# An encoder kernel's inner norms: second statistics as sums and squares, more late modulation units ahead of the norm, and constants loaded later

## The chip, the cores and the metric

The kernel runs on one core of a Trainium2 chip. The metric is the device time of one execution in microseconds (us), the median of several runs. The engines are TensorE (PE in the profile, PEld for its weight loads), VectorE (DVE), ScalarE (ACT), GpSimd (POOL) and SyncE (SP), whose queue issues most of the DMA transfers. Each takes its own list of instructions.

## The reference

Two layers of an encoder for 256 tokens of 2048 columns, all in float32. Cut to what matters here:

```python
for l in range(2):
    mod = (silu(c) @ w_mod[l] + b_mod[l]).reshape(bn, 6, d)       # shift_m, scale_m, gate_m, shift_f, scale_f, gate_f
    h = layer_norm(x) * (1.0 + scale_m) + shift_m
    proj = h @ w_in[l]                                            # 4288 columns
    y_a, y_b, y_c, y_d = ...                                      # gMLP, latent attention, short conv, conformer conv
    y = concatenate([y_a, y_b, y_c, y_d]) @ w_out[l]
    x = layer_norm(ALPHA * x + (1.0 + gate_m) * y, post_mix_g[l], post_mix_b[l])
    h = layer_norm(x) * (1.0 + scale_f) + shift_f
    y = conv_ffn(h, w_up, w_conv, b_conv, w_down)                 # 2048 -> 2 x 5632 -> 2048
    x = layer_norm(ALPHA * x + (1.0 + gate_f) * y, post_ffn_g[l], post_ffn_b[l])
```

At the end of each half of a layer two layer norms follow each other: one with gain and bias that makes the new x, and at once a plain one that makes the input of the next half. The second needs the mean and the variance of what the first has written. I call the three places where both follow each other the inner norms: o0 (after layer 0's output projection), d0 (after layer 0's feed-forward) and o1 (after layer 1's output projection). After d1 only the first norm is left, and the output is stored.

## The kernel before

**Products.** The weights come from memory in tiles of 1 MB (`raw`, a ring of four, `weights()`). A tile is split into a rounded part and a remainder, in fp32r: ScalarE casts `whi` (or `thi`), VectorE subtracts `wlo` (or `tlo`), and TensorE makes three products for each pair. The activations are split likewise (`hT`, `a`). Where a call says `exact`, the weights are loaded into the places of the halves instead (`wexact`), and TensorE makes one fp32 product, which it does in two records; ScalarE and VectorE then have nothing to do. In `out_proj` of layer 0, `plain={1024: 2, 1536: 4}` says which units are exact: two of the four of the column block at 1024, and all four of the block at 1536.

**Order.** `stream()` issues the load of one unit and puts its products off until after the load of the next. The order on each engine follows the order of the code, as a scheduler settles it from dependences; each engine then runs its list in order.

**Modulation.** `c @ w_mod` is made by VectorE (`mod_step`: one multiply-add per 128 rows, into `macc` or `qacc`) and summed over the partitions by TensorE (`ps_mod`). It goes on in the background: after each unit of weights `pump()` adds the rate of the phase (`RATES`) to a credit, and takes that many units of `mod_stream`. Layer 0's SHIFT_F and SCALE_F are first done up to column 1536; their last 512 columns are the eight late units (four of SHIFT_F, four of SCALE_F, each with 1 MB and four operations of 128x512). Before the change they begin after the norm o0: `load_late_first()` loads the first two into slots, and the rest follow in the phase "first". `needs()` settles the sums, `late()` those of the late columns.

**The start.** x is loaded and normed, and layer 0's SHIFT_M and SCALE_M are made in five pieces of columns (`piece()`, `PIECES`), while the products D, U, V and E use the columns that are done (`by_pieces()`). The constants `cst` beyond the first 128 columns and the parameter rows (`load_rows`, ten transfers of at most 64 KB) are issued on GpSimd's queue at the very start. The rows are turned by TensorE (`ps_rows`) after the second piece.

**The inner norms.** `out_proj` ends with a block of 512 columns, whose last four units are put off: TensorE makes their products for token tile 0 (128 tokens) first, then for tile 1. So the norm of tile 0 (`finish`, then `norm`) runs under the products of tile 1. For each tile VectorE multiplies with the gate (`yg`, L692), adds the residual (L695), takes statistics (L698), and then passes over the four quarters of x: `(x - mean) * gain` (L715), `* rstd + bias` (L718), and `bn_stats` of the result (L724). `rstd_of` makes the mean and 1/std of these second statistics (L562, L564, GpSimd's power on L112, L567), the pair r. From r ScalarE makes `xn` (L86), TensorE transposes it (`ps_xT`), ScalarE (tile 0) or VectorE (tile 1) writes `hF` with scale and shift, and the products of the next half begin (`first_group`: `g_c` after o0 and o1, `U_c` after d0).

Of the kernel before, what the change touches and what calls it, by code (L numbers as in the profile page):

```python
# [13 lines left out]
P = 128  # L14
# [40 lines left out]
def encoder_kernel(ctx: ExitStack, tc: tile.TileContext, A: dict, consts: bass.AP, out: bass.AP):  # L55
# [52 lines left out]
    mhalf = keep.tile([P, 4], F32, name="mhalf")  # L108
    pool.memset(mhalf, -0.5)

    def power(o, i):
        pool.tensor_tensor(out=o, in0=i, in1=mhalf[:, : i.shape[1]], op=ALU.pow)  # L112

# [11 lines left out]
    cact = keep.tile([P, 16], F32, name="cact")  # L125
    dve.tensor_copy(cact, pst[:, 0:16])

    def load_rows(parts, n, dst):

        r = smallp.tile([P, P], F32, tag="rows", name="rows", bufs=5)  # L130
        at = 0
        for ap in parts:
            pool.dma_start(out=r[at : at + ap.shape[0], :], in_=ap)
            at += ap.shape[0]
        assert at == n

        def turn():
            ps = ms_tile("ps_rows")
            pe.transpose(ps[:, 0:n], r[0:n, :], ident[0:n, 0:n])
            dve.tensor_copy(dst, ps[:, 0:n])  # L140

        return turn

    def rows(ap):
        if len(ap.shape) == 1:
            return ap.rearrange("(j p) -> j p", p=P)
        return ap.rearrange("k (j p) -> (k j) p", p=P)
# [4 lines left out]
        bcol.append(b)  # L152
    turn_b0 = load_rows([rows(A["b_mod"][0])], 96, bcol[0])

    pool.dma_start(out=cst[:, 128:1024], in_=consts[:, 128:1024])

    PM = []
    PF = []
    for l in range(DEPTH):
# [2 lines left out]
        PM.append(pm)  # L162
        PF.append(pf)

    def load_params(l):
        turns = []
        if l > 0:
            turns.append(load_rows([rows(A["b_mod"][l])], 96, bcol[l]))
        turns.append(load_rows([rows(A["conf_w_dw"][l])], 124, PM[l][:, 0:124]))
        turns.append(  # L170
            load_rows(
                [
                    rows(A["mla_q_norm"][l]),
                    rows(A["mla_kv_norm"][l]),
                    rows(A["sconv_w"][l]),
                    rows(A["conf_b_dw"][l]),
                    rows(A["conf_ln_g"][l]),
                    rows(A["conf_ln_b"][l]),
                ],
                29,  # L180
                PM[l][:, 124:153],
            )
        )
        wc = rows(A["ffn_w_conv"][l])
        turns.append(load_rows([wc[0:128]], 128, PF[l][:, 0:128]))
        turns.append(load_rows([wc[128:132], rows(A["ffn_b_conv"][l])], 48, PF[l][:, 128:176]))
        return turns


# [120 lines left out]
        )  # L310
        return [dst[:, k * 512 : (k + 1) * 512] for k in range(nk)]

    late_first = {}

    def load_late_first():
        for v in (SHIFT_F, SCALE_F):
            late_first[v] = late_part(0, v, 0, 2, slot("wlate")) + late_part(0, v, 2, 2, slot("wlate"))

    def mod_stream(order):

        held_back = {}
        for l, m in order:
            if (l, m) == (0, GATE_F):

                for u in range(4):
                    for v, acc in held_back.items():
                        ws = late_first[v] if u == 0 else late_part(u, v, 0, 4, raw_tile("wmod"))
                        for k in range(4):  # L330
                            mod_step(acc[:, LATE_KT * P :], ws[k], 4 * u + k, u + k == 0)
                        if u == 3:
                            late.append((0, v, acc, LATE_KT, KT))
                        yield
# [319 lines left out]
    def out_proj(l, w, src, order, gate_of, name, post_g, post_b, before, then, plain={}, bg=0):  # L654
# [45 lines left out]
        def gains():  # L700
            gb = []
            for row in (post_g, post_b):
                r = raw_tile("gb")
                nc.sync.dma_start(out=r, in_=row.partition_broadcast(P))
                gb.append(r)
            box["gb"] = gb

        def norm(t):
            gb = box["gb"]
            mv, r = rstd_of(stats[t], f"{name}p{t}", False)  # L710
            st2 = new_stats(f"{name}q{t}")
            for q in range(4):
                cols = slice(q * 512, (q + 1) * 512)
                xs = X[t][:, cols]
                dve.scalar_tensor_tensor(  # L715
                    out=xs, in0=xs, scalar=mv[:, 0:1], in1=gb[0][:, cols], op0=ALU.subtract, op1=ALU.mult
                )
                dve.scalar_tensor_tensor(  # L718
                    out=xs, in0=xs, scalar=r[:, 0:1], in1=gb[1][:, cols], op0=ALU.mult, op1=ALU.add
                )  # L720
                if then is None:
                    nc.sync.dma_start(out=out[0, t * P : (t + 1) * P, cols], in_=xs)
                else:
                    dve.bn_stats(out=st2[:, q, :], in_=xs)  # L724
            if then is not None:
                _, box[t] = rstd_of(st2, f"{name}r{t}", True)

        for c0, width in CHUNKS:
            last = c0 + width == D
# [722 lines left out]
    for l in range(DEPTH):  # L1452
# [4 lines left out]
        else:  # L1457
# [97 lines left out]
```

## Time and profile before

| | |
|---|---|
| median of 3 runs | 2304.81 us (2304.12 to 2306.32) |
| the profiled execution | 2308.31 us, its span 2306.5 us |
| TensorE, busy share of the span | 97% |
| VectorE | 78% |
| ScalarE | 46% |
| GpSimd | 2% |
| mean granted clock of TensorE | 0.987 |

The profile comes from one execution. A row of the timeline reads: start (us from the span's start), duration, engine, line, operation, out<-in, shape, and in brackets how long the engine was idle before it and what ended that. A row of the list of waits reads: who waited, for whom, total us, times, the longest. A row of a stretch reads: from:to, length, then busy us and (instructions) of PE, PEld, DVE, ACT and POOL, the granted clock, the DMA engines' busy share and GB/s.

### The profile page before, as it was taken

To read this page: it belongs to the slowest core of one execution; us is meant where nothing else is said; L and a number is where in the kernel's file an instruction comes from. 1 tells how busy PE (TensorE), PEld (TensorE's weight loads), DVE (VectorE), ACT (ScalarE), POOL (GpSimd) and SP (SyncE) were. 2 spreads that over 40 slices of the span, in tenths; PEclk is the share of its full clock that TensorE was granted. 3 is DMA by queue.
4 is the path that set the end of the run, shared out by engine and by line. 5 is a ranking of instruction groups with operands and counts; after the bars stand their busy time and mean duration, and the time that the engine had idled before them with its cause. 6 is when DMAs were issued, how large, how long until landed. Compare 5 with 4: busy or idle time off the path is not lost. (4 is left out here: it accounts for less than half of the span.)

```text
span 2306.5 us, 31422 instructions
## 1 busy us (share of the span) xinstructions
PE 2240.3 (97%) x12387; PEld 1937.9 (84%) x12387; DVE 1788.2 (78%) x2181; ACT 1062.5 (46%) x1573; POOL 34.7 (2%) x64
## 2 busy tenths in 40 slices
PE   6899999999999999999999999999999999999998
PEld 4688886688888888888789989879888888888886
DVE  6878987778888888987977799887676555565676
ACT  2235742235454544544445435535454454454553
POOL 1000000000000000000000000000000000000000
PEclk9999999999999999999999999999999999999999
DMA  9999788777889888898857667775766555555554
GB/s 343 353 342 342 270 322 330 262 272 284 305 305 335 295 325 323 298 348 304 317 185 249 207 220 258 281 272 183 250 241 215 184 183 201 184 193 190 184 198 146
DMA packets 228717, 605.21 MB, mean 262 GB/s; under 512 B 14660, under 2 KB 27188, under 8 KB 210900
## 3 DMA queue, kind: packets, MB, share of 16 engines
q1 hardware_dynamic: 227784, 602.30, 73.6%
q8 instruction: 97, 1.59, 0.3%
q0 software_dynamic: 784, 0.90, 0.1%
q14 instruction: 52, 0.43, 0.1%
HBM read 601.05 MB, written 2.10 MB: 261 GB/s over the span
## 5 line engine op out<-in xcount | busy, mean ns | idle before, releaser
L451 ACT CAST whi<-wraw 128x1024 fp32r<-128x1024 f32 (+1 forms) x632 | 643.9, 1043 | 783.2 <-PE g_c L83 210.7
L452 DVE TENSOR_TENSOR wlo<-wraw,whi 128x1024 fp32r<-128x1024 f32 (+1 forms) x632 | 751.2, 1214 | 302.8 <-ACT whi L451 285.4
L83 PE MATMUL d<-whi,a 128*128 128x512 f32 x1344 | 390.0, 391 | 0.9 <-ACT whi L451 0.9
L246 DVE SCALAR_TENSOR_TENSOR macc<-wmod,cact,macc 128x2048 f32<-128x2048 f32 (+2 forms) x174 | 353.8, 2034 | 31.6 <-DMA wmod<-in_w_mod_dram 31.0
L83 PE MATMUL v_c<-hT,whi 128*128 128x512 f32 (+1 forms) x1456 | 343.1, 383 | 0.0
L83 PE MATMUL g_c<-hT,whi 128*128 128x512 f32 (+1 forms) x1344 | 313.3, 380 | 0.0
L83 PEld LDWEIGHTS v_c<-hT,whi 128*128 128x128 f32 x1456 | 264.6, 189 | 48.5
L83 PEld LDWEIGHTS d<-whi,a 128*128 128x128 f32 x1344 | 253.2, 189 | 54.5 <-ACT whi L451 2.2
L83 PEld LDWEIGHTS g_c<-hT,whi 128*128 128x128 f32 x1344 | 243.4, 189 | 43.2
L83 PE MATMUL d<-wlo,a 128*128 128x512 f32 x672 | 234.9, 392 | 1.7 <-DVE wlo L452 1.6
L83 PE MATMUL v_c<-hT,wlo 128*128 128x256 f32 x1400 | 190.7, 283 | 0.0
L83 PEld LDWEIGHTS v_c<-hT,wlo 128*128 128x128 f32 x1400 | 183.2, 191 | 6.6
L83 PE MATMUL g_c<-hT,wlo 128*128 128x256 f32 x1280 | 175.8, 283 | 0.0
L83 PEld LDWEIGHTS g_c<-hT,wlo 128*128 128x128 f32 x1280 | 168.2, 191 | 5.9
L83 PEld LDWEIGHTS d<-wlo,a 128*128 128x128 f32 x672 | 127.0, 189 | 30.0 <-DVE wlo L452 3.6
L471 ACT CAST a<-g 128x512 fp32r<-128x512 f32 x132 | 80.6, 619 | 86.4 <-PE d L83 84.7
L83 PE MATMUL o<-whi,a 128*128 128x512 f32 x384 | 112.3, 397 | 0.8 <-ACT whi L451 0.8
L472 DVE TENSOR_TENSOR a<-g,a 128x512 fp32r<-128x512 f32 x132 | 88.0, 684 | 9.0 <-ACT a L471 9.0
L83 PEld LDWEIGHTS o<-whi,a 128*128 128x128 f32 x384 | 73.2, 191 | 17.3 <-issue 1.2
L83 PE MATMUL D_c<-hT,whi 128*128 128x256 f32 x432 | 82.0, 290 | 2.8 <-ACT hT L471 2.3
L246 DVE SCALAR_TENSOR_TENSOR qacc<-wmod,cact,qacc 128x1024 f32<-128x1024 f32 (+1 forms) x75 | 80.3, 1070 | 2.7 <-DMA wmod<-in_w_mod_dram 0.6
L83 PEld LDWEIGHTS D_c<-hT,whi 128*128 128x128 f32 x432 | 69.5, 197 | 4.7 <-ACT hT L471 2.6
(328 smaller groups left out, 2599.6 us busy)
## 6 DMA issues: line engine op xcount, KB each, us to landing
wraw<-in_ffn_w_up_dram SPq DMA_DIRECT2D x168, 1024.0 KB, 5.1
wmod<-in_w_mod_dram SPq DMA_DIRECT2D x134, 1024.0 KB, 6.5
wraw<-in_ffn_w_down_dram SPq DMA_DIRECT2D x88, 1024.0 KB, 5.2
wraw<-in_w_in_dram SPq DMA_DIRECT2D x33, 1024.0 KB, 5.6
wmod<-in_w_mod_dram SPq DMA_DIRECT2D x64, 512.0 KB, 8.7
wraw<-in_w_out_dram SPq DMA_DIRECT2D x26, 1024.0 KB, 6.9
wmod<-in_w_mod_dram SPq DMA_DIRECT2D x32, 768.0 KB, 7.0
wexact<-in_w_in_dram SPq DMA_DIRECT2D x46, 512.0 KB, 7.1
```

Of the source, the lines that this page charges most:

```text
L83: pe.matmul(o, lhsT, rhs, start=start, stop=stop, skip_group_check=True)
L246: i = dve.scalar_tensor_tensor(out=acc, in0=w, scalar=col, in1=acc, op0=ALU.mult, op1=ALU.add)
L451: act.copy(hi[:, :m], r)
L452: i = dve.tensor_tensor(out=lo[:, :m], in0=r, in1=hi[:, :m].bitcast(F32), op=ALU.subtract)
L471: act.copy(hi, src)
L472: dve.tensor_tensor(out=lo, in0=src, in1=hi.bitcast(F32), op=ALU.subtract)
```

## The change

It has five parts.

1. Inner norms: `second(t)` takes the place of `norm(t)`. The offset pass writes its sum too (`accum_out`), ScalarE squares the result about c and sums the squares (`sq`), and six small operations on VectorE make mean and variance of them. c is minus the mean of the bias row, made by `gains()` from four statistics for each inner norm.
2. `RATES` for layer 0's output projection goes from 1.7 to 1.95. In its twelve units with modulation that is three more units, which are the first three late ones. `load_late_first()` then loads the two that follow these.
3. In layer 0's output projection the two exact units of the block at 1024 are split like others.
4. The rest of `cst` and layer 0's rows are issued on SP's queue at the fourth call of `piece` (made at the start of the third piece), and the rows are turned after the last piece.
5. A constant tile `eps`.

```diff
-    dict(B=1.6, C=1.9, out=1.7, first=1.2, up=0.68, down=0.83),
+    dict(B=1.6, C=1.9, out=1.95, first=1.2, up=0.68, down=0.83),
...
+    eps = keep.tile([P, 1], F32, name="eps")
+    pool.memset(eps, LN_EPS)
...
-    def load_rows(parts, n, dst):
+    def load_rows(parts, n, dst, by=pool):
...
-            pool.dma_start(out=r[at : at + ap.shape[0], :], in_=ap)
+            by.dma_start(out=r[at : at + ap.shape[0], :], in_=ap)
...
-    pool.dma_start(out=cst[:, 128:1024], in_=consts[:, 128:1024])
...
+    LATE_UNITS = [(u, v) for u in range(4) for v in (SHIFT_F, SCALE_F)]
+    late_first, late_taken = {}, []
     def load_late_first():
-        for v in (SHIFT_F, SCALE_F):
-            late_first[v] = late_part(0, v, 0, 2, slot("wlate")) + late_part(0, v, 2, 2, slot("wlate"))
+        n = len(late_taken)
+        for u, v in LATE_UNITS[n : n + 2]:
+            late_first[u, v] = late_part(u, v, 0, 2, slot("wlate")) + late_part(u, v, 2, 2, slot("wlate"))
...
+            if then is None:
+                return
+            st = new_stats(f"{name}b")
+            for q in range(4):
+                dve.bn_stats(out=st[:, q, :], in_=gb[1][:, q * 512 : (q + 1) * 512])
+            mb = smallp.tile([P, 2], F32, tag="mv", name=f"mv_{name}b", bufs=4)
+            dve.bn_aggr(out=mb, in_=st)
+            box["c"] = keep.tile([P, 1], F32, tag="negc", name=f"c_{name}")
+            dve.tensor_scalar(out=box["c"], in0=mb[:, 0:1], scalar1=-1.0, scalar2=None, op0=ALU.mult)
+
+        def second(t):
+            gb, c = box["gb"], box["c"]
             mv, r = rstd_of(stats[t], f"{name}p{t}", False)
-            st2 = new_stats(f"{name}q{t}")
+            sums = smallp.tile([P, 4, 6], F32, tag="stats", name=f"st_{name}q{t}", bufs=4)
             for q in range(4):
...
                 dve.scalar_tensor_tensor(
+                    out=xs, in0=xs, scalar=r[:, 0:1], in1=gb[1][:, cols], op0=ALU.mult, op1=ALU.add,
+                    accum_out=sums[:, q, 0:1],
+                )
+                act.activation(
+                    out=tmp_tile("sq"), in_=xs, func=AF.Square, bias=c, accum_out=sums[:, q, 1:2]
+                )
+            m = smallp.tile([P, 6], F32, tag="m2", name=f"m_{name}{t}")
+            dve.tensor_reduce(out=m[:, 0:1], in_=sums[:, :, 0], axis=AX.X, op=ALU.add)
+            dve.tensor_scalar(out=m[:, 1:2], in0=m[:, 0:1], scalar1=1.0 / D, scalar2=None, op0=ALU.mult)
+            dve.tensor_scalar(out=m[:, 2:3], in0=m[:, 1:2], scalar1=c, scalar2=None, op0=ALU.add)
+            dve.scalar_tensor_tensor(
+                out=m[:, 3:4], in0=m[:, 2:3], scalar=m[:, 2:3], in1=eps, op0=ALU.mult, op1=ALU.subtract
+            )
+            dve.tensor_reduce(out=m[:, 4:5], in_=sums[:, :, 1], axis=AX.X, op=ALU.add)
+            dve.scalar_tensor_tensor(
+                out=m[:, 5:6], in0=m[:, 4:5], scalar=1.0 / D, in1=m[:, 3:4], op0=ALU.mult, op1=ALU.subtract
+            )
+            r = smallp.tile([P, 2], F32, tag="rs", name=f"rs_{name}r{t}", bufs=4)
+            power(r[:, 0:1], m[:, 5:6])
+            last_norm[0] = dve.scalar_tensor_tensor(
+                out=r[:, 1:2], in0=m[:, 1:2], scalar=-1.0, in1=r[:, 0:1], op0=ALU.mult, op1=ALU.mult
+            )
+            box[t] = r
...
-                if then is None:
-                    nc.sync.dma_start(out=out[0, t * P : (t + 1) * P, cols], in_=xs)
-                else:
-                    dve.bn_stats(out=st2[:, q, :], in_=xs)
-            if then is not None:
-                _, box[t] = rstd_of(st2, f"{name}r{t}", True)
+                nc.sync.dma_start(out=out[0, t * P : (t + 1) * P, cols], in_=xs)
...
-                    norm(t)
+                    (norm if then is None else second)(t)
...
-            turns.extend(load_params(0))
+        if q == 3:
+            nc.sync.dma_start(out=cst[:, 128:1024], in_=consts[:, 128:1024])
+            turns.extend(load_params(0, nc.sync))
...
-            if q == 1:
+            if q == 4:
                 for turn in turns:
                     turn()
...
-            plain={1024: 2, 1536: 4} if l == 0 else {},
+            plain={1536: 4} if l == 0 else {},
```

Where the instructions stand now is seen at three places. First ScalarE at the inner norm o1, before the change: behind the last cast of the projection's weights come `xn` of tile 0 (x0) and its `hF`.

```order
L451 CAST whi_12542<-wraw_12536 128x1024
L86 ACTIVATE xn_12728<-x0_95,rs_o1r0_12674 128x512
L86 ACTIVATE xn_12739<-x0_95,rs_o1r0_12674 128x512
L86 ACTIVATE hF0_12546<-ps_xT_12730,mod_1_3_6182,mod_1_4_7424 128x128 x4
L86 ACTIVATE hF1_12547<-ps_xT_12741,mod_1_3_6182,mod_1_4_7424 128x128 x4
```

The same place after the change (`sq` are the squares, `st_o1q0` and `st_o1q1` the sums of the two tiles):

```order
L742 ACTIVATE sq_12767,st_o1q0_12764<-x0_97,c_o1_12609 128x512
L742 ACTIVATE sq_12771,st_o1q0_12764<-x0_97,c_o1_12609 128x512
L742 ACTIVATE sq_12775,st_o1q0_12764<-x0_97,c_o1_12609 128x512
L742 ACTIVATE sq_12779,st_o1q0_12764<-x0_97,c_o1_12609 128x512
L742 ACTIVATE sq_12803,st_o1q1_12800<-x1_98,c_o1_12609 128x512
L742 ACTIVATE sq_12807,st_o1q1_12800<-x1_98,c_o1_12609 128x512
L742 ACTIVATE sq_12811,st_o1q1_12800<-x1_98,c_o1_12609 128x512
L742 ACTIVATE sq_12815,st_o1q1_12800<-x1_98,c_o1_12609 128x512
L86 ACTIVATE xn_12849<-x0_97,rs_o1r0_12788 128x512
L86 ACTIVATE xn_12860<-x0_97,rs_o1r0_12788 128x512
L86 ACTIVATE xn_12887<-x0_97,rs_o1r0_12788 128x512
L86 ACTIVATE hF0_12651<-ps_xT_12851,mod_1_3_6253,mod_1_4_7495 128x128 x4
```

The eight squares stand ahead of the first `xn`, those of tile 1 (x1) too, and a third `xn` of tile 0 stands ahead of its first `hF`. It is the same at o0 and d0.

Second, VectorE at the same norm, tile 0, before the change:

```order
L715 SCALAR_TENSOR_TENSOR x0_95<-x0_95,mv_o1p0_12654,gb_12502 128x512 x2
L718 SCALAR_TENSOR_TENSOR x0_95<-x0_95,rs_o1p0_12656,gb_12504 128x512 x2
L724 BN_STATS st_o1q0_12659<-x0_95 128x6 x2
L562 BN_AGGR mv_o1r0_12672<-st_o1q0_12659 128x2
L564 TENSOR_SCALAR rs_o1r0_12674<-mv_o1r0_12672 128x1
L567 SCALAR_TENSOR_TENSOR rs_o1r0_12674<-mv_o1r0_12672,rs_o1r0_12674 128x1
L692 TENSOR_TENSOR yg_12678<-o1_153610_12521,gate_1_2_12163 128x512
```

and after it:

```order
L733 SCALAR_TENSOR_TENSOR x0_97,st_o1q0_12764<-x0_97,rs_o1p0_12761,gb_12600 128x512 x2
L746 TENSOR_REDUCE m_o10_12781<-st_o1q0_12764 128x1
L747 TENSOR_SCALAR m_o10_12781<-m_o10_12781 128x1
L748 TENSOR_SCALAR m_o10_12781<-m_o10_12781,c_o1_12609 128x1
L749 SCALAR_TENSOR_TENSOR m_o10_12781<-m_o10_12781,eps_95 128x1
L752 TENSOR_REDUCE m_o10_12781<-st_o1q0_12764 128x1
L753 SCALAR_TENSOR_TENSOR m_o10_12781<-m_o10_12781 128x1
L758 SCALAR_TENSOR_TENSOR rs_o1r0_12788<-m_o10_12781,rs_o1r0_12788 128x1
L697 TENSOR_TENSOR yg_12791<-o1_153610_12626,gate_1_2_12259 128x512
```

The statistics are gone, small operations have come, and `yg` of tile 1 follows directly behind tile 0's last small operation as before.

Third, SP's queue between the last weights of E in the second piece and the first of D in the third, before the change:

```order
L429 DMA wexact_480<-in_w_in_dram 128x2x512
L437 DMA wraw_527<-in_w_in_dram 128x2x1024
L261 DMA wmod_537<-in_w_mod_dram 128x2x512 x2
L261 DMA wmod_542<-in_w_mod_dram 128x2x512 x2
L261 DMA wmod_547<-in_w_mod_dram 128x2x512 x2
```

and after it:

```order
L434 DMA wexact_455<-in_w_in_dram 128x2x512
L1463 DMA cst_82<-in_consts_dram 128x896
L136 DMA rows_503<-in_conf_w_dw_dram 124x128
L136 DMA rows_505<-in_mla_q_norm_dram 3x128
L136 DMA rows_505<-in_mla_kv_norm_dram 2x128
L136 DMA rows_505<-in_sconv_w_dram 12x128
...
L136 DMA rows_514<-in_ffn_w_conv_dram 4x128
L136 DMA rows_514<-in_ffn_b_conv_dram 44x128
L442 DMA wraw_517<-in_w_in_dram 128x2x1024
```

Eleven transfers have come between E's weights and `wraw`, and the modulation weights of the third piece follow behind them.

More of the change, by code (lines that the diff above doesn't have):

```diff
@@ L163, in encoder_kernel, with load_params @@
         PF.append(pf)
-    def load_params(l):
+    def load_params(l, by=pool):
         turns = []
         if l > 0:
-            turns.append(load_rows([rows(A["b_mod"][l])], 96, bcol[l]))
-        turns.append(load_rows([rows(A["conf_w_dw"][l])], 124, PM[l][:, 0:124]))
+            turns.append(load_rows([rows(A["b_mod"][l])], 96, bcol[l], by))
+        turns.append(load_rows([rows(A["conf_w_dw"][l])], 124, PM[l][:, 0:124], by))
         turns.append(
@@ L181, in load_params @@
                 PM[l][:, 124:153],
+                by,
             )
@@ L184, in load_params @@
         wc = rows(A["ffn_w_conv"][l])
-        turns.append(load_rows([wc[0:128]], 128, PF[l][:, 0:128]))
-        turns.append(load_rows([wc[128:132], rows(A["ffn_b_conv"][l])], 48, PF[l][:, 128:176]))
+        turns.append(load_rows([wc[0:128]], 128, PF[l][:, 0:128], by))
+        turns.append(load_rows([wc[128:132], rows(A["ffn_b_conv"][l])], 48, PF[l][:, 128:176], by))
         return turns
@@ L311, in late_part @@
         return [dst[:, k * 512 : (k + 1) * 512] for k in range(nk)]
-    late_first = {}
+    LATE_UNITS = [(u, v) for u in range(4) for v in (SHIFT_F, SCALE_F)]
+    late_first, late_taken = {}, []
     def load_late_first():
-        for v in (SHIFT_F, SCALE_F):
-            late_first[v] = late_part(0, v, 0, 2, slot("wlate")) + late_part(0, v, 2, 2, slot("wlate"))
+        n = len(late_taken)
+        for u, v in LATE_UNITS[n : n + 2]:
+            late_first[u, v] = late_part(u, v, 0, 2, slot("wlate")) + late_part(u, v, 2, 2, slot("wlate"))
     def mod_stream(order):
@@ L325, in mod_stream @@
             if (l, m) == (0, GATE_F):
[L327 to L334, printed above, removed]
+                for u, v in LATE_UNITS:
+                    acc = held_back[v]
+                    late_taken.append((u, v))
+                    ws = late_first.get((u, v)) or late_part(u, v, 0, 4, raw_tile("wmod"))
+                    for k in range(4):
+                        mod_step(acc[:, LATE_KT * P :], ws[k], 4 * u + k, u + k == 0)
+                    if u == 3:
+                        late.append((0, v, acc, LATE_KT, KT))
+                    yield
             while len(late) >= 2:
@@ new lines, in second @@
+        def second(t):
+            gb, c = box["gb"], box["c"]
+            mv, r = rstd_of(stats[t], f"{name}p{t}", False)
+            sums = smallp.tile([P, 4, 6], F32, tag="stats", name=f"st_{name}q{t}", bufs=4)
+            for q in range(4):
+                cols = slice(q * 512, (q + 1) * 512)
+                xs = X[t][:, cols]
+                dve.scalar_tensor_tensor(
+                    out=xs, in0=xs, scalar=mv[:, 0:1], in1=gb[0][:, cols], op0=ALU.subtract, op1=ALU.mult
+                )
+                dve.scalar_tensor_tensor(
+                    out=xs,
+                    in0=xs,
+                    scalar=r[:, 0:1],
+                    in1=gb[1][:, cols],
+                    op0=ALU.mult,
+                    op1=ALU.add,
+                    accum_out=sums[:, q, 0:1],
[7 more added lines that the diff above has]
+            dve.tensor_scalar(out=m[:, 2:3], in0=m[:, 1:2], scalar1=c, scalar2=None, op0=ALU.add)
+            dve.scalar_tensor_tensor(
+                out=m[:, 3:4], in0=m[:, 2:3], scalar=m[:, 2:3], in1=eps, op0=ALU.mult, op1=ALU.subtract
+            )
+            dve.tensor_reduce(out=m[:, 4:5], in_=sums[:, :, 1], axis=AX.X, op=ALU.add)
+            dve.scalar_tensor_tensor(
+                out=m[:, 5:6], in0=m[:, 4:5], scalar=1.0 / D, in1=m[:, 3:4], op0=ALU.mult, op1=ALU.subtract
[4 more added lines that the diff above has]
+                out=r[:, 1:2], in0=m[:, 1:2], scalar=-1.0, in1=r[:, 0:1], op0=ALU.mult, op1=ALU.mult
+            )
+            box[t] = r
```

## The prediction

> **What bounds the kernel.** I read the page's busy shares first, then the list of waits of TensorE alone, then the timeline around the places that this list names.
>
> ```profile
> span 2306.5 us, 31422 instructions
> PE 2240.3 (97%) x12387; PEld 1937.9 (84%) x12387; DVE 1788.2 (78%) x2181; ACT 1062.5 (46%) x1573; POOL 34.7 (2%) x64
> ```
>
> TensorE (PE) works 97% of the span. Only three things can change the time: its work, its clock, and the some 66 us in which it stands idle. The waits say where it stands (line, what ended the wait, total us, times, longest):
>
> ```profile
> PE ps_xT L1397 <- ACT xn L86: 13.0, 2, 12.8
> PE ps_xT L585 <- ACT xn L86: 9.0, 5, 3.1
> PE E L83 <- DMA wexact<-in_w_in_dram: 4.4, 1, 4.4
> PE ps_mod L83 <- DVE macc L246: 2.2, 1, 2.2
> ```
>
> The first row is the kernel's start. The second is the inner norms (o0, d0, o1), which stop TensorE for 3.1 us at most: the norm of token tile 0 runs under the tail products of token tile 1, and the norm of tile 1 under the first products of tile 0. The change touches every one of these four rows.
>
> **The inner norms: what now releases TensorE.** The norm o1 in the timeline, VectorE and GpSimd, then ScalarE, then TensorE:
>
> ```profile
> 1540.79 0.69 DVE L692 TENSOR_TENSOR yg<-o,gate 128x512 f32<-128x512 f32 x1 [1.93 <-PE o L83]
> ...
> 1543.34 1.40 DVE L715 SCALAR_TENSOR_TENSOR x<-x,mv_o1p,gb 128x512 f32<-128x512 f32 x2
> 1544.66 1.41 DVE L718 SCALAR_TENSOR_TENSOR x<-x,rs_o1p,gb 128x512 f32<-128x512 f32 x2
> 1545.98 1.28 DVE L724 BATCH_NORM_STATS2 st_o1q<-x 128x6 f32<-128x512 f32 x2
> ...
> 1551.43 0.15 DVE L564 TENSOR_SCALAR rs_o1r<-mv_o1r 128x1 f32<-128x1 f32 x1
> 1552.26 0.16 DVE L567 SCALAR_TENSOR_TENSOR rs_o1r<-mv_o1r,rs_o1r 128x1 f32<-128x1 f32 x1 [0.67 <-POOL rs_o1r L112]
> 1552.34 0.69 DVE L692 TENSOR_TENSOR yg<-o,gate 128x512 f32<-128x512 f32 x1
> ...
> 1554.88 1.41 DVE L715 SCALAR_TENSOR_TENSOR x<-x,mv_o1p,gb 128x512 f32<-128x512 f32 x2
> ...
> 1551.66 0.56 POOL L112 TENSOR_TENSOR rs_o1r<-rs_o1r,mhalf 128x1 f32<-128x1 f32 x1 [7.17 <-DVE rs_o1r L564]
> ...
> 1552.45 1.52 ACT L86 ACTIVATE xn<-x,rs_o1r 128x512 f32<-128x512 f32 x2 [15.03 <-DVE rs_o1r L567]
> 1554.02 2.90 ACT L86 ACTIVATE hF<-ps_xT,mod,mod 128x128 f32<-128x128 f32 x8
> ...
> 1549.88 0.39 PE L83 MATMUL o<-whi,a 128*128 128x512 f32 x1
> 1553.32 1.36 PE L585 MATMUL ps_xT<-cst,xn 128*128 128x128 f32 x8 [3.06 <-ACT xn L86]
> 1554.53 3.84 PE L83 MATMUL g_c<-hF,wexact 128*128 128x128 f32 x32
> ```
>
> Today ScalarE sits idle for 15.03 us and starts xn of tile 0 at 1552.45, 0.11 us after VectorE has gone on to tile 1 (yg, 1552.34). Two scaling passes take 1.32 us from start to start (0.66 each); two second statistics take 1.28, 0.60 each without the overlap that the passes' 1.41 shows too.
>
> The change takes the four second statistics of a tile off VectorE (4 x 0.60 = 2.4 us) and puts four squares per tile on ScalarE. In ScalarE's order all eight squares, those of tile 1 too, stand ahead of xn of tile 0. ScalarE takes its work in order, so xn of tile 0, and with it hF, the casts of the next weights, and TensorE's transposes and products, wait until VectorE has finished both passes over tile 1. I cost that for o1, with these prices for a square and for the read of its sum:
>
> ```profile
> L873 ACT ACTIVATE sqD<-convD x4: 630/631/632, 320.4 to 1454.2; 128x512 f32<-128x512 f32 x4
> L1103 ACT ACTIVATION_READ_ACCUMULATOR p<-ps_sc,sm,rr x16: 189/194/206, 275.6 to 1409.0; 128x1 f32 x16
> ```
>
> - Tile 0 on VectorE: passes from 1543.34, 8 x 0.66 = 5.28, so 1548.6; last square and read 0.82; then a reduction and one small operation (0.18 each, after the 0.15 row; the four before them hide under the square), GpSimd's power 0.56 and the last small operation with three hand-overs, together some 1.3: 1550.7. Tile 1 starts there, 1.65 us earlier than today. That is the gain meant.
> - Tile 1: 2.54 us from yg to the passes (1552.34 to 1554.88), 5.28 of passes, 0.82 for the last square and its read, 0.1 to hand over: xn of tile 0 starts 8.74 us after yg, at 1559.45, against 1552.45. That is 7.0 us late.
> - Three xn now stand ahead of the first hF where two did: 0.76 more. First products 7.75 us late.
>
> For d0 and o0 the same sum, but the tail products of tile 1 end later than the shorter chain of tile 0, so yg of tile 1 starts right behind them (1213.9 and 434.0):
>
> ```profile
> 1213.49 0.39 PE L83 MATMUL d<-whi,a 128*128 128x512 f32 x1
> ...
> 1214.75 1.52 ACT L86 ACTIVATE xn<-x,rs_d0r 128x512 f32<-128x512 f32 x2 [15.28 <-DVE rs_d0r L567]
> ...
> 430.37 3.60 PE L83 MATMUL o<-wexact,yd 128*128 128x512 f32 x8
> ...
> 435.49 1.52 ACT L86 ACTIVATE xn<-x,rs_o0r 128x512 f32<-128x512 f32 x2 [21.93 <-DVE rs_o0r L567]
> ```
>
> d0: 1213.95 + 8.74 = 1222.7 against 1214.75, and 0.76: 8.7 us. o0: 442.75 against 435.49, and 0.76: 8.0 us. The three norms: **+24.5 us**. Nothing behind gives it back: from there to the next norm TensorE has its products back to back.
>
> The offset pass now also writes a sum. No row shows what that costs on VectorE; 0 and ScalarE's 0.19 for such a read bound it. Four of tile 1 count in each norm and four of tile 0 in o1, 16 in all: 0 to 3.0 us; between the ends I take 0.1 each, **+1.6**. The Trainium skill (VectorE: DVE Perf Modes, "Two Vector instructions with no wait between them") says that an operation that also writes its accumulator is two instructions, the main one and a read. By it the upper end, 3.0, would be the value; no run here shows it yet.
>
> The memset of eps is one more on an idle GpSimd: 0. The bias statistics (4 x 0.60 and two small ones per norm) run while VectorE waits for tail products (1.93 us idle in the first row above, more with the 2.4 taken off): 0.
>
> **The clock.** A longer stop also costs clock. Windows of 3.4 us; the number behind POOL's is the granted clock:
>
> ```profile
> 1213.70:1217.20 3.50, 1.71 (x12) 1.21 (x12) 2.64 (x8) 2.40 (x5) 0.55 (x1) 1.00 0.94 300
> 1217.20:1220.70 3.50, 3.50 (x20) 3.50 (x19) 3.50 (x7) 3.42 (x8) 0.92 (x1) 0.51 1.05 396
> ...
> 1551.80:1555.30 3.50, 1.93 (x14) 1.61 (x15) 2.90 (x7) 2.80 (x6) 0.68 (x2) 1.00 1.03 385
> ```
>
> Half a window of work at d0 brought 0.51 for the next 3.5 us, 1.7 us lost; 1.93 of 3.50 at o1 did not. With stops of some 10 us each norm should lose 1.7; d0 does already: **+3.4** (0 to 8, if it takes three windows as at the late rows below). The Trainium skill (TensorE: Matmul & The Clock Gate, "Why this matters for your kernels") asks for no idle gap above about 3 us. By that d0's short stop would have cost nothing today and the three norms would add 5.1; here the trace disagrees with it at d0.
>
> **The start.** Constants and rows leave the start, where they share the DMA engines with x, and come back on SP's queue at the third piece.
>
> ```profile
> 2.20 0.59 POOL L155 DMA_DIRECT2D cst<-in_consts_dram  x1
> 14.32 0.49 DVE L244 TENSOR_SCALAR qacc<-wmod,cact 128x512 f32<-128x512 f32 x1 [0.25 <-DMA wmod<-in_w_mod_dram]
> ...
> 33.62 6.68 PE L83 MATMUL D_c<-hF,wexact 128*128 128x256 f32 x16
> ...
> 69.45 0.42 SPq L429 DMA_DIRECT2D wexact<-in_w_in_dram  x1
> 71.59 0.37 SPq L437 DMA_DIRECT2D wraw<-in_w_in_dram  x1
> ```
>
> 0.63 MB at 385 GB/s (the last figure of the last row above) is 1.6 us; GpSimd's power no longer stands behind its DMA issues, and one copy of hF goes ahead of the first qacc. VectorE is the limit from 14.32 on, so the first products come up to 3.6 us earlier. At 69.45 eleven small transfers (0.42 us of issue each, 4.6 us) now stand between E's weights and the next wraw, which had 2.1 us to spare: I give back 1.1. **-2.5** (-3.6 to +0.5).
>
> **Layer 0's output projection.** Two units go from exact fp32 to split: 16 products of two records each at 3.60/8 = 0.43 (the row of yd), 0.86 each, become 48 at 0.227 (the split products of d in the chain that ended last):
>
> ```profile
> 2053.61 119.70 PE d L83 x528
> ```
>
> 13.7 against 10.9, -2.8. Against it stand 8 splits on VectorE and ScalarE (four wlo at 1.2 = 4.9 us) and three more units of modulation before the norm (3 MB, and 12 operations of 0.74).
>
> ```profile
> 365.00:380.00 15.00, 14.53 (x51) 11.45 (x52) 11.43 (x10) 3.28 (x4) 0.00 (x0) 0.81 0.67 242
> 380.00:390.00 10.00, 10.00 (x24) 4.38 (x24) 9.97 (x13) 0.54 (x1) 0.00 (x0) 1.00 1.03 401
> 390.00:400.00 10.00, 10.00 (x34) 6.21 (x33) 7.28 (x6) 3.04 (x4) 0.00 (x0) 1.00 0.97 341
> ```
>
> VectorE has 3.6 + 2.7 us free here and the DMA 33% of 15 us; 13.8 us of VectorE and 8.6 us of DMA come in, part of it after 400. So some 2 of the 2.8 us go back: **-1** (-2.8 to +6).
>
> **The late columns.** Three of eight units are done before the norm, so the sums after it no longer wait:
>
> ```profile
> 499.82 1.33 PE L83 MATMUL ps_mod<-onesR,macc 128*128 128x1 f32 x8 [2.18 <-DVE macc L246]
> ...
> 506.00:508.00 2.00, 2.00 (x6) 1.62 (x5) 2.00 (x3) 0.98 (x2) 0.00 (x0) 0.50 0.43 165
> ```
>
> 2.18 us go, and perhaps a third of the some 3 us that half clock costs behind it: **-3.2** (0 to -6).
>
> **Sum:** 24.5 + 1.6 + 3.4 - 2.5 - 1 - 3.2 = +22.8 us on the profiled execution (2308.31 with what lies around its span), which is 3.5 above the median of the three runs. On the median, 2304.81: **2327.6 us**, 1% slower. The norms' 24.5 I hold to 2 us; the ends of all terms together are +10 to +44.
>
> **Rivals.**
> 1. *The norms do get shorter* (faster). xn of tile 0 starts on tile 0's own numbers. With the other terms at -2.5, -1 and -3.2 this decides from a delay of xn under some 2 us a norm. With none, o1 gains 1.65, d0 0.7 and o0 1.3 (today's xn less 0.11, against the new yg): 2304.8 - 3.6 - 6.7 = 2294.5. For it: the chain of tile 0 really loses 2.4 us. Against it: the order on ScalarE. 0.07.
> 2. *The output projection starves as well.* DMA and VectorE are late with the fourth unit's halves, and the tail waits: +6 in place of -1, 2334.6. For it: ScalarE already waits for wraw there; against it: the 33% free. 0.18, slower.
> 3. *The stop is there but earlier and later gains cancel it*: it needs the low ends of all and more, 2304.8 +- 4.6. 0.04.
> The forecast has the rest, 0.71. A difference under 0.2% (4.6 us) could not be told from none. Slower holds 0.71 + 0.18 = 0.89, faster 0.07, the same 0.04. The forecast's own range is 2316 to 2335; with rival 2 above it, 2314 to 2339 leaves out about 2 in 10.
>
> **What would show it.** Right: TensorE's wait for xn at each inner norm 9 to 12 us instead of 1.8 to 3.1, with ScalarE's idle time ahead of tile 1's squares ended by VectorE; tile 1's yg about 1 us earlier behind tile 0; half clock behind each norm; the first D_c products near 30; no wait of ps_mod for macc near 500. Wrong: xn of tile 0 within 1 us of its own last small operation, or the eight squares ending before VectorE's tile 1 passes do.

## The result and the profile after

The changed kernel takes 2330.97 us (median of 4 runs, 2329.44 to 2333.14) against 2304.47 us before (4 runs, 2302.04 to 2306.32): a ratio of 1.0117, 95% interval 1.0105 to 1.0129, so 26.5 us slower. The forecast was 2327.6 us, with a range of 2314 to 2339. The profiled execution took 2333.14 us.

The busy shares of the page after the change:

```profile
span 2331.4 us, 31580 instructions
PE 2244.3 (96%) x12403; PEld 1944.6 (83%) x12403; DVE 1792.6 (77%) x2227; ACT 1084.8 (47%) x1625; POOL 29.6 (1%) x54
```

and TensorE's list of waits (line, what ended the wait, total us, times, longest):

```profile
PE ps_xT L590 <- ACT xn L86: 31.0, 4, 10.4
PE ps_xT L1446 <- ACT xn L86: 7.8, 2, 7.3
...
PE V L83 <- DMA wexact<-in_w_in_dram: 5.3, 2, 3.7
...
PE E L83 <- DMA wexact<-in_w_in_dram: 4.2, 1, 4.2
PE o L83 <- ACT whi L456: 4.0, 3, 2.0
```

TensorE does the same work (2244.3 against 2240.3 us, part of the difference being half clock). The wait of the inner norms has gone from 9.0 to 31.0 us; that of the start (L1446) fell from 13.0 to 7.8. The row of `ps_mod` for `macc` is gone, and two rows are new or larger: `V` waits 5.3 us for weights where it waited 2.0, and `o` waits for casts.

The norm o1 in the timeline of the changed kernel, VectorE, then ScalarE, then TensorE:

```profile
1558.86 1.41 DVE L730 SCALAR_TENSOR_TENSOR x<-x,mv_o1p,gb 128x512 f32<-128x512 f32 x2
...
1566.22 0.16 DVE L758 SCALAR_TENSOR_TENSOR rs_o1r<-m_o,rs_o1r 128x1 f32<-128x1 f32 x1 [0.67 <-POOL rs_o1r L115]
1566.30 0.68 DVE L697 TENSOR_TENSOR yg<-o,gate 128x512 f32<-128x512 f32 x1
...
1573.51 0.75 DVE L733 SCALAR_TENSOR_TENSOR x<-x,rs_o1p,gb 128x512 f32<-128x512 f32 x1
1574.18 0.09 DVE L733 DVE_READ_ACCUMULATOR x<-x,rs_o1p,gb 128x1 f32 x1
...
1571.01 0.72 ACT L742 ACTIVATE sq<-x,c_o 128x512 f32<-128x512 f32 x1 [5.85 <-DVE x L733]
...
1575.02 0.19 ACT L742 ACTIVATION_READ_ACCUMULATOR sq<-x,c_o 128x1 f32 x1
1575.11 2.21 ACT L86 ACTIVATE xn<-x,rs_o1r 128x512 f32<-128x512 f32 x3
1577.22 2.87 ACT L86 ACTIVATE hF<-ps_xT,mod,mod 128x128 f32<-128x128 f32 x8
...
1575.96 1.97 PE L590 MATMUL ps_xT<-cst,xn 128*128 128x128 f32 x8 [10.39 <-ACT xn L86]
1577.72 5.59 PE L83 MATMUL g_c<-hF,wexact 128*128 128x128 f32 x32
```

The mean and 1/std of tile 0 are there at 1566.38 (1566.22 and 0.16). `xn` of tile 0 needs nothing else, but starts at 1575.11, at the last read of tile 1's squares. ScalarE has been idle for 5.85 us, 4.6 of them in this time, when tile 1's first square begins: it waits, with that square at its head, for VectorE's pass over tile 1.

Where the 24.8 us between the two profiled executions lie, by the starts and ends of TensorE's product groups in the two traces:

| stretch | before, us | after, us | difference |
|---|---|---|---|
| start to the first product of `o` in layer 0 | 328.33 | 326.51 | -1.82 |
| layer 0's output projection | 105.63 | 107.98 | +2.35 |
| norm o0: last `o` to first `g_c` | 3.60 | 11.47 | +7.87 |
| first `g_c` to first `d` (late columns, half clock) | 519.58 | 516.78 | -2.80 |
| norm d0: last `d` to first `U_c` | 2.95 | 11.47 | +8.52 |
| norm o1: last `o` to first `g_c` | 4.26 | 12.15 | +7.89 |
| first `g_c` to first `d`, layer 1 (half clock) | 498.92 | 500.69 | +1.77 |
| all others | | | +1.06 |

### The profile page after: what moved, and what is told of

It is laid out like the page before. It is cut to its first block, busy times and chain, and to the rows that moved or that the text cites. A ratio compares the mean times of both kernels' runs of the same rounds, so it can differ in the third digit from the quotient of the medians.

```text
span 2331.4 us, 31580 instructions
## 1 busy us (share of the span) xinstructions
PE 2244.3 (96%) x12403; PEld 1944.6 (83%) x12403; DVE 1792.6 (77%) x2227; ACT 1084.8 (47%) x1625; POOL 29.6 (1%) x54
## 4 chain that ended last, share of the span: by engine, by line
PE 88%; DVE 6%; DMA 3%; ACT 2%; issue 1%; POOL 0%; SPq 0%; DVEq 0%; ACTq 0%; POOLq 0%
PE g_c L83 22%; PE v_c L83 21%; PE d L83 20%; PE C_c L83 4%; PE D_c L83 4%; PE o L83 3%; PE B_c L83 3%; DVE wlo L457 1%; PE U_c L83 1%; PE E L83 1%; PE ps_mod L83 1%; PE E_c L83 1%; DVE macc L248 1%; DVE qacc L248 1%; PE V L83 1%
## 5 line engine op out<-in xcount | busy, mean ns | idle before, releaser
L248 DVE SCALAR_TENSOR_TENSOR macc<-wmod,cact,macc 128x2048 f32<-128x2048 f32 (+2 forms) x172 | 352.4, 2051 | 39.4 <-DMA wmod<-in_w_mod_dram 38.7
L83 PE MATMUL o<-whi,a 128*128 128x512 f32 x416 | 123.4, 399 | 4.1 <-ACT whi L456 4.0
L83 PEld LDWEIGHTS o<-whi,a 128*128 128x128 f32 x416 | 79.1, 191 | 23.2 <-ACT whi L456 5.5
L248 DVE SCALAR_TENSOR_TENSOR qacc<-wmod,cact,qacc 128x1024 f32<-128x1024 f32 (+1 forms) x75 | 80.3, 1071 | 5.2 <-DMA wmod<-in_w_mod_dram 3.0
L83 PE MATMUL o<-wlo,a 128*128 128x512 f32 x208 | 73.7, 404 | 0.2 <-DVE wlo L457 0.2
```

What stands on the lines that cost most here:

```text
L83: pe.matmul(o, lhsT, rhs, start=start, stop=stop, skip_group_check=True)
L248: i = dve.scalar_tensor_tensor(out=acc, in0=w, scalar=col, in1=acc, op0=ALU.mult, op1=ALU.add)
```

## The experiments

Ratios are to the kernel before, run beside it on the same chip, with 95% intervals. 0.001 is 2.3 us.

### The statistics alone, and the other parts alone

`n1_second_alone` is the kernel before with `second()`, the statistics of the bias row and `eps`; `n2_old_norm` is the changed kernel with the `norm` of before for both tiles:

```diff
-                    (norm if then is None else second)(t)
+                    norm(t)
```

> The kernel before with nothing but the new second statistics of the inner norms. Theory A (the order on ScalarE: tile 1's squares stand ahead of xn of tile 0): all three stops of TensorE near 10 us, first products 24.3 us later in all as in the changed kernel, half clock behind them 4 us more: +28 us, 2333 us, if the late columns gain only from the higher rate of units; +23 to +26, 2328 to 2331, if the stop by itself gives the late loads their time. Rival (the loss comes from the other parts, the stop is taken back later): within 5 us of before.

> The changed kernel with the statistics of before (bn_stats on VectorE) in the inner norms; start, rate and split units as changed. Theory A: the stops are back at 2 to 3 us. Start -1.8, output projection +2.3, late columns -4.8 if the three units ahead give it: 2300 us; if the late columns gained only because of the stop: 2305. Rival (the other parts do the harm): 2310 us or more.

Measured: `n1_second_alone` 2330.53 us, 1.0115 (1.010 to 1.013); `n2_old_norm` 2306.38 us, 1.0012 (1.0002 to 1.0021). The statistics by themselves cost all of it, +26.5 us; the other parts, for which the prediction had -6.7 us together, cost 2.8 (0.5 to 4.8). The two add up to 29 against 26.9 for the whole, which lies within the intervals. The wait of `ps_mod` for `macc` stays at 1.81 us in the trace of `n1_second_alone`, so the stop alone does not remove it. Its time lies at the upper end of the range that was given for the case that it does (2328 to 2331), 2.5 us under the other, so the time doesn't tell the two apart.

### Order or chain: one tile at a time

In `n3_tile1_stats` tile 1 keeps `bn_stats`, in `n4_tile0_stats` tile 0 does:

```diff
-                    (norm if then is None else second)(t)
+                    (norm if then is None or t == 1 else second)(t)      # n3
+                    (norm if then is None or t == 0 else second)(t)      # n4
```

> The changed kernel, but tile 1 has its statistics by bn_stats on VectorE as before; tile 0 keeps sums and squares. Nothing of tile 1 then stands on ScalarE ahead of xn of tile 0. Theory A (order): xn of tile 0 starts within 0.3 us of its own last small operation, TensorE's stops are 0.5 to 1.5 us at each inner norm, 2 to 4 us less than the old statistics in all: 2296 us (2293 to 2300). Rival B (the new chain of tile 0 is itself slow: reads of sums, hand-overs between engines): the stops stay near 10 us, 2325 us or more.

> The mirror: tile 0 has bn_stats as before, tile 1 sums and squares. Tile 1's four squares stand ahead of xn of tile 0. Theory A (order): xn still waits for VectorE's passes over tile 1, the stops are 9 to 11.5 us (at o1 some 1 us longer than in the changed kernel, since tile 0's chain is longer again): 2331 us (2327 to 2336). Rival B (tile 0's new chain is slow): the stops are back at 2 to 3 us, 2300 to 2305.

Measured: `n3_tile1_stats` 2300.63 us, 0.9981 (0.9970 to 0.9991); `n4_tile0_stats` 2335.71 us, 1.0134 (1.0117 to 1.0151). The norm o1 of the first on ScalarE, and of the second on TensorE:

```profile
1543.61 0.19 ACT L742 ACTIVATION_READ_ACCUMULATOR sq<-x,c_o 128x1 f32 x1
1545.11 1.52 ACT L86 ACTIVATE xn<-x,rs_o1r 128x512 f32<-128x512 f32 x2 [1.31 <-DVE rs_o1r L758]
```

```profile
1579.04 1.97 PE L590 MATMUL ps_xT<-cst,xn 128*128 128x128 f32 x8 [11.89 <-ACT xn L86]
```

With tile 0's own squares alone ahead of it, `xn` starts when tile 0's last small operation ends. With tile 1's alone ahead of it, though tile 0 has nothing new, the stop is 11.89 us, 1.5 more than in the changed kernel: the old chain of tile 0 is longer by about that, and everything of tile 1 comes later. So the new chain is the shorter one, and only the place of tile 1's squares costs. The rival (the new chain itself is slow) falls twice. `n3_tile1_stats` is some 4 us above what was expected, since its other parts gain nothing.

### The same work in another order

`f1_ordered` is the whole change. Tile 1's squares and small operations are put off into `box["rest"]`, which `first_group` calls after the third quarter of tile 0:

```diff
-                act.activation(
-                    out=tmp_tile("sq"), in_=xs, func=AF.Square, bias=c, accum_out=sums[:, q, 1:2]
-                )
+                if t == 0:
+                    square(sums, xs, q)
+            if t == 0:
+                moments(sums, 0)
+                return
+            last_norm[0] = i
+            def rest():
+                for q in range(4):
+                    square(sums, X[1][:, q * 512 : (q + 1) * 512], q)
+                moments(sums, 1)
+            box["rest"] = rest
...
             if n + 1 < len(steps):
                 turned(*steps[n + 1])
+            if n == 1:
+                r.pop("rest")()
```

`f2_ordered_exact` also has `plain={1024: 2, 1536: 4}` of before. `b2_tile0_alone` is the kernel before with the norm of `n3_tile1_stats` and nothing else.

> The whole change; only the place of tile 1's four squares on ScalarE differs: they are written after the third quarter of tile 0's xn and its small operations with them. The same work on every engine. Theory A (the order is the whole loss): stops of 0.8 to 1.8 us at the inner norms, no half clock behind them; as fast as the kernel with tile 1's statistics by bn_stats or up to 1 us faster, 0.998 to 0.9975 of the time before (-4 to -6 us). Rival (the squares themselves, or the reads of their sums, cost on ScalarE wherever they stand): stops of 3 us or more, no faster than before.

> As the run with the squares moved, and the two units of the projection's block at 1024 exact as before. Theory A (three more units of modulation and the split of two units crowd ScalarE's casts together): the projection 1.5 us shorter, 0.9975 to 0.9965 of the time before (-6 to -8 us). Rival (the split is free): equal to the run with the squares moved.

> The kernel before with nothing but sums and squares for tile 0 of the inner norms; tile 1 keeps bn_stats. Theory A: 1.3 us at o1, some 1.5 at o0, 1.7 at d0 and the half clock behind d0's stop: -5 us, 0.998 of the time before (0.9985 to 0.997). Rival (the shorter norm is lost again because the next stage waits for weights or splits): within 0.0005 of 1.

Measured: `f1_ordered` 2300.92 us, 0.9982 (0.9973 to 0.9991); `f2_ordered_exact` 2298.67 us, 0.9963 (0.9949 to 0.9976); `b2_tile0_alone` 2294.36 us, 0.9953 (0.9940 to 0.9965). TensorE's waits at the inner norms in `f1_ordered`, and o1 there on ScalarE:

```profile
PE ps_xT L590 <- ACT xn L86: 4.8, 6, 1.8
```

```profile
1540.78 1.52 ACT L86 ACTIVATE xn<-x,rs_o1r 128x512 f32<-128x512 f32 x2 [1.31 <-DVE rs_o1r L778]
1542.34 2.91 ACT L86 ACTIVATE hF<-ps_xT,mod,mod 128x128 f32<-128x128 f32 x8
1545.10 0.85 ACT L86 ACTIVATE xn<-x,rs_o1r 128x512 f32<-128x512 f32 x1
1545.80 0.76 ACT L759 ACTIVATE sq<-x,c_o 128x512 f32<-128x512 f32 x1
```

The same instructions on every engine, with eight squares still on ScalarE, take 1.0117 of the time before in one order and 0.9982 in the other. The order is the whole loss. Taking tile 1 off VectorE too brings nothing over tile 0 alone (`f1_ordered` against `n3_tile1_stats`), since nothing waits for tile 1's statistics for long. The fastest of all is the kernel before with tile 0's statistics changed and nothing else: 10.9 us (8 to 14) faster than before, twice what was expected, and some 37 faster than the changed kernel.

### The small parts one by one

`p1_rate_alone`, `p2_split_alone` and `p3_start_alone` are the kernel before with one part each: the rate of 1.95 with the late units, `plain={1536: 4}`, and the constants and rows on SP's queue at the third piece (the diff of the change, cut to that part).

> The kernel before with nothing but the higher rate in layer 0's output projection and the late units that follow from it. Theory A (the three units ahead of the norm give the late columns their gain): no wait of ps_mod for macc behind o0, the late stage 3 to 4.8 us shorter, the projection up to 1 us longer: -3 us, 2301.5 us (2300 to 2303.5). Rival (in the changed kernel the stop at the norm gave the late loads their time): the wait of some 2 us stays, 2304.5 to 2306.

> The kernel before with nothing but the two exact units of the block at 1024 split. Theory A (the prediction's step: 2.8 us of products less, little given back while the rate is 1.7): -1.5 us, 2303 us (2301.8 to 2304). Rival (splits are late here: ScalarE's casts wait for their turn, TensorE waits for whi): TensorE stands 2 to 3 us for whi in the projection as in the changed kernel, +1 us, 2305 to 2307.

> The kernel before with nothing but the constants and rows moved to SP's queue at the third piece. First products of D near 32 against 33.6 us, E and V wait as long as in the changed kernel: -1.8 us, 2302.7 us (2301 to 2304), as the changed kernel shows at its first product of the output projection. Rival (the eleven transfers take it back): 2304 to 2306.

Measured: 1.0002 (0.9993 to 1.0011), 1.0010 (1.0000 to 1.0020) and 1.0003 (0.9995 to 1.0012). None of the three gains anything that can be told; theory A was too good by 2.5 to 4 us in each. `p2_split_alone` fits its rival: TensorE stands 2.4 us in the projection, though for weights, `wlo` and `whi` by 0.8 each. The three add up to 1.0015, near the 1.0012 of `n2_old_norm`.

### The clock, with the stop filled

`p4_fill` is the changed kernel with work for TensorE in the stops:

```diff
+                if then is not None:
+                    ps = ms_tile("ps_fill")
+                    for k in range(NFILL):                       # 11
+                        i = mm(ps, ident, cst[:, 512:1024], k == 0, k == NFILL - 1)
+                        tc.add_manual_dep(i.ins, last_mm[0].ins.name, order_dep, reason="behind the last products")
```

> The changed kernel, with 11 fp32 products of 128x512 of constants (9.4 us by 0.857 us each) on TensorE in each of the three stops, between the last products of token tile 1 and the transposes; nobody reads them. The stop stays as long; only TensorE's idleness goes. Theory A (idle time brings half clock): no half clock behind the norms, transposes 1.36 us again instead of 1.97; 0.55 us of first products and some 2 us behind them come back at each: -6 us, 2325 us (2323 to 2327). Rival (half clock comes from something else, or the filled stop only puts it off): 2330 to 2332.

Measured: 2324.53 us, 1.0091 (1.0077 to 1.0104), against 1.0117 for the changed kernel: some 6 us (2 to 10) come back. Its norm o1 on TensorE:

```profile
1556.06 9.61 PE L85 MATMUL ps_fill<-cst 128*128 128x512 f32 x22
1566.61 1.36 PE L592 MATMUL ps_xT<-cst,xn 128*128 128x128 f32 x8 [0.94 <-ACT xn L88]
1568.36 3.84 PE L85 MATMUL g_c<-hF,wexact 128*128 128x128 f32 x32 [0.40 <-ACT hF L88]
```

The transposes and products are back at 1.36 and 3.84 us, where the changed kernel has 1.97 and 5.59. The three stretches from the last product to the first of the next half are as long as they were (11.46, 11.46 and 12.14 us against 11.47, 11.47 and 12.15), so the clock's part of the loss is shown apart from the stop's.

## Why the prediction was right, step by step

**The norms' delay, +24.5: right, +24.3.** By the table above 7.9 at o0 (forecast 8.0), 8.5 at d0 (8.7) and 7.9 at o1 (7.75). The two pieces it was made of hold as well: tile 0's passes to tile 1's `yg` took 7.44 us (1558.86 to 1566.30, forecast 7.36), tile 1's `yg` to `xn` 8.81 (1566.30 to 1575.11, forecast 8.74). The third `xn` ahead of `hF` cost 0.5, not 0.76: in `p4_fill`, at full clock, the first products come 1.75 us behind the transposes' start, in the kernel before 1.21.

**The sum on VectorE, +1.6: too high, some +0.2.** The read is an instruction of its own, as the Trainium skill says (VectorE: DVE Perf Modes, "Two Vector instructions with no wait between them"), but it runs beside the next one. The pass with the sum and its reads in the changed kernel:

```profile
1570.16 0.75 DVE L733 SCALAR_TENSOR_TENSOR x<-x,rs_o1p,gb 128x512 f32<-128x512 f32 x1
1570.84 0.08 DVE L733 DVE_READ_ACCUMULATOR x<-x,rs_o1p,gb 128x1 f32 x1
1570.84 0.75 DVE L733 SCALAR_TENSOR_TENSOR x<-x,rs_o1p,gb 128x512 f32<-128x512 f32 x1
1571.51 0.09 DVE L733 DVE_READ_ACCUMULATOR x<-x,rs_o1p,gb 128x1 f32 x1
1571.51 1.41 DVE L730 SCALAR_TENSOR_TENSOR x<-x,mv_o1p,gb 128x512 f32<-128x512 f32 x2
```

From start to start it is 0.67 to 0.68 against 0.66 without a sum, 0.01 to 0.02 for each of the 16. That a pair costs the sum of both was the prediction's own step: its 3.0 is 16 times ScalarE's 0.19, for reads that stand in the line by themselves, and none here does.

**The clock, +3.4: right in kind, too high.** In the last part of the long stops and behind them the granted clock is 0.50, here at d0 and at o1:

```profile
1223.00:1233.00 10.00, 3.72 (x17) 3.53 (x18) 6.49 (x19) 7.51 (x19) 0.86 (x2) 0.50 1.02 392
...
1576.00:1579.00 3.00, 3.00 (x14) 2.81 (x15) 0.16 (x1) 3.00 (x8) 0.21 (x1) 0.50 1.00 373
1579.00:1582.00 3.00, 3.00 (x18) 3.00 (x18) 0.78 (x1) 3.00 (x7) 0.00 (x0) 0.59 0.34 131
```

The Trainium skill asks for no idle gap above about 3 us (TensorE: Matmul & The Clock Gate, "Why this matters for your kernels"): with the long stops (9.7 to 10.4 us) the traces agree, with the short ones below they do not. The first 32 products of 3.84 us took 4.90, 4.89 and 5.59 at o0, d0 and o1, 3.86 us more. What was wrong is what the kernel before loses already, of which I counted 1.7 us at d0 alone. In the five kernels with the old statistics that were traced (before, `n2_old_norm`, and the three with small parts) 12 of the 15 short stops have a window of 3.4 us at half clock at their end or behind them; the profiled execution before had 1 of 3. One of the others, `p1_rate_alone`, at o0:

```profile
434.00:437.50 3.50, 1.06 (x8) 0.73 (x8) 2.63 (x7) 1.84 (x3) 0.56 (x1) 1.00 0.98 330
437.50:441.00 3.50, 3.50 (x20) 3.42 (x18) 3.43 (x8) 3.27 (x9) 0.99 (x1) 0.57 1.02 380
```

By the same measure, the first 32 products, these five lose 2.71 us on average and the profiled execution before 1.63. So the long stops added 1.2 us to the one and 2.2 to the other, not 3.4. In the four kernels in which `xn` of tile 0 waits for tile 0 alone (stops of 0.83, 0.25 and 1.78 us) and in `p4_fill` none of the 15 norms is followed by one. So `b2_tile0_alone` gains 4.3 us by its shorter stops (2.40, 1.75 and 3.06 before) and, as an estimate, 3 to 4 by the 2.4 such windows that it avoids on average. The rest of its 10.9 us is open; its mean clock over five executions is 0.990, that of before 0.987.

**The start, -2.5: wrong.** D's first products come at 32.21, not near 30, and E's wait is still 4.2 us. The gain was mis-sized (1.4 us at D, where 3.6 was the most), and so was the 1.1 us given back to the eleven transfers: `V`'s wait for weights behind them rose by 3.3 us:

```profile
101.14 3.75 PE L83 MATMUL V<-wexact,hF 128*128 128x512 f32 x4 [3.67 <-DMA wexact<-in_w_in_dram]
```

Eight traces with this part reach the first product of `o` at 325.9 us on average, five without it at 326.5, both within 323 to 329, and the time of `p3_start_alone` is at 1.0003. Its mean clock over 11 executions is 0.985 against 0.987 before, and 0.002 of 2300 us is 4.6 us, enough for the 2.5 us between the -1.8 expected of it and what was measured; that this is the cause is not shown. Half clock in the first 175 us comes to 30 us on average in the eight traces (24 to 34), 21 in the five (10 to 27). Why is not shown either; that the moved loads leave a longer stop there (the 6.7 us in the list of waits for `qacc`, 2.4 before) was not tried apart.

**Layer 0's output projection, -1: wrong in sign, +2.4.** The step that failed is the room that was read from the stretches before, "VectorE has 3.6 + 2.7 us free here and the DMA 33% of 15 us": with the work that comes in both are full, and the casts come late. Three stretches after the change:

```profile
370.00:380.00 10.00, 8.01 (x31) 5.61 (x32) 10.00 (x10) 2.00 (x2) 0.00 (x0) 1.00 0.98 381
380.00:390.00 10.00, 10.00 (x40) 7.24 (x39) 10.00 (x11) 2.00 (x2) 0.00 (x0) 1.00 0.95 326
390.00:400.00 10.00, 10.00 (x41) 7.41 (x40) 9.76 (x11) 2.00 (x2) 0.00 (x0) 1.00 0.97 333
```

and around the first of them SP's queue, ScalarE and TensorE:

```profile
368.31 0.38 SPq L442 DMA_DIRECT2D wraw<-in_w_out_dram  x1
...
375.68 2.00 ACT L456 CAST whi<-wraw 128x1024 fp32r<-128x1024 f32 x2 [6.11 <-DVE x L700]
382.07 2.00 ACT L456 CAST whi<-wraw 128x1024 fp32r<-128x1024 f32 x2 [4.40 <-DMA wraw<-in_w_out_dram]
...
376.77 0.73 PE L83 MATMUL o<-whi,a 128*128 128x512 f32 x2 [1.99 <-ACT whi L456]
```

The row of the first cast names VectorE's residual of the block before (L700), which ended in the same moment. The cast's own weights fit better: the transfer issued at 368.31, when a modulation step of VectorE (L248) had just ended, landed at 375.58 by the trace's record of it, 0.10 us ahead of the cast, and the next cast stands as far behind the landing of its own (381.97). TensorE then waited 1.99 us for the cast. VectorE is busy for 9.8 to 10.0 of each 10 us here and the DMA engines at 0.95 to 0.98; which of the two holds the weights up is not shown. This was rival 2 in kind, with a smaller price. From first to last product the projection takes 104.8 to 106.2 us in four traces with neither, 105.2 and 107.0 with the rate alone, 107.8 with the split alone, and 107.7 to 109.1 in six with both. Not all of that is waiting: half clock within the projection comes to 6.0 us on average in the four and to 9.1 in the six, and at most half of that difference, 1.6 us, is lost by it, of the 2.6 us between their means. Left exact, in `f2_ordered_exact`, the two units bring some 4 us (0.7 to 8) over `f1_ordered`.

**The late columns, -3.2: too high, some -1.** The wait of `ps_mod` for `macc` is gone in all kernels with the higher rate, and stands at 1.8 to 2.2 us in four of the five without. The time follows it only in part. The stretch from `g_c` to `d` is 3.7 us shorter than in `n1_second_alone`, which has the same stops, but that trace has 14.6 us at half clock in it and the changed kernel 9.1. With half of the time at half clock taken off, as an estimate of what it costs, the stretch takes 512.2 us in the changed kernel and 513.2 in `n1_second_alone`, and with short stops 512.3 in `p1_rate_alone` against 513.4 and 513.3 in the other two with one small part. As they stand the last three are 517.4, 517.6 and 517.5, and no gain is seen. Over all traces the estimate gives 512.2 to 513.1 us in seven with the higher rate (an eighth, `f2_ordered_exact`, has 516.1, with 2.5 us more of other waits) and 513.2 to 514.5 in the five without. So the three units bring some 1 us, behind a long stop as behind a short one.

**The sum.** The prediction was 3.4 us under the result, nearer than its terms, and that is in part luck. The small parts were 9.5 us too good (-6.7 against +2.8); the statistics by themselves, forecast at +29.5, cost 26.5, and the two parts measured apart add up to 2.4 more than the whole, which the intervals allow. Rival 1 was decided as it said, by the delay of `xn`: once the order was changed (`f1_ordered`) the three norms were 4.3 us shorter together than before (1.6 at o0, 1.5 at d0, 1.3 at o1), where it had 3.65 (1.3, 0.7 and 1.65).

## What to carry to other kernels

Before moving work to an idle engine, look at what stands behind it in that engine's order and when its input is ready: an engine that is 53% idle can still hold up the bound for 8 us with four operations of 0.7. Take the work off the path for the part that is waited for (here tile 0) and leave the rest where it is, or put it behind what is waited for. A gain read from free shares in one stretch, and a clock read from one execution, are to be checked against several traces.

## What was not expected of the hardware

Half clock also comes in the middle of work. In layer 0's down projection TensorE is busy without a gap by the profile, and still the clock falls, at about the same place in the program before the change and after it (two stretches, the first of before):

```profile
1060.00:1070.00 10.00, 10.00 (x51) 9.12 (x50) 4.22 (x4) 2.68 (x4) 0.00 (x0) 0.68 0.76 287
```

```profile
1070.00:1080.00 10.00, 10.00 (x39) 8.55 (x39) 4.91 (x4) 3.00 (x5) 0.00 (x0) 0.69 0.65 232
```

The other traces have 3.4 or 6.8 us of it there, but for one (`n2_old_norm`) with none. No run here tells what brings it. And the stop of 1.78 us at o1, in the four kernels named above, was never followed by half clock, while one of 1.75 at d0 was in four of five: the length of the stop alone does not settle it.
